# The causal mask inside VectorE's scan, and the carried product without GpSimd: stick-breaking attention in a hybrid decoder layer

## The chip, the core and the metric

The kernel runs on one core of a Trainium2 chip. The metric is the device time of one execution in microseconds (us), from several runs of each kernel on the same chip; smaller is better. The engines are TensorE (PE; PEld are its weight loads), VectorE (DVE), ScalarE (ACT) and GpSimd (POOL); SyncE (SP) issues most DMAs, GpSimd those that feed the attention.

## What is computed

One layer over a prompt of 2048 tokens with 16 meta tokens before them, and over 8 sequences that each add 8 tokens to a cache of 512. A norm, one input projection, then side by side a stick-breaking attention (8 heads of 64) and a gated linear recurrence; an output projection, a norm, an MLP of squared ReLU, a norm. The attention is what the change touches:

```python
z = einsum(q, k) * HEAD_DIM**-0.5 + bias
mask = k_pos[None, :] < q_pos[:, None]
log_keep = where(mask, log_sigmoid(-z), 0.0)
suffix = lax.cumsum(log_keep, axis=3, reverse=True) - log_keep
w = where(mask, exp(log_sigmoid(z) + suffix), 0.0)
out = einsum(w, v)
```

A key's weight is sigmoid(z) times the product of (1 - sigmoid(z')) over all later keys that the query may see. A query sees neither its own key nor later ones.

## The kernel before

The sequence is four blocks `s` of 512 tokens. For each block the projections run first (`inproj`: recurrence, keys, values, queries), and the attention of finished blocks is mixed into later work: `attn` and `sample_attn` are generators, and each GEMM hands them a little time after every few of its products (`work.tick`, with rates written out by hand). TensorE's order is exactly the order in which the program is written; a scheduler orders the other engines. Matrix products take three passes each (high by high, low by high, high by low, lines 181 to 183 and 213 to 215), and the weights are split on the way: ScalarE casts the high part (L158), VectorE subtracts the low part (L159).

In `attn`, work goes head by head and from the latest group of 512 keys to the earliest. For a 128-row tile of queries, `logits` (L692) makes two products into a PSUM tile S (L696). Where the tile holds the rows' own keys, a third product adds -2^100 to the masked places: the identity `identb` times the table `maskb`, both bf16 (L698). There are 4 such tiles for each head of each block, 128 in all. Then `chain` (L629) has ScalarE compute keep = sigmoid(-z) and beta = sigmoid(z) (L634, L635). VectorE scans keep from the last key to the first, each element the product so far (L643), into `pb`, starting from 1 or from the `carry` of the later group, and multiplies beta with the scan's element one place to the right (L646). That one place further, the last column of `pb`, is filled by GpSimd: a memset of 1 (L637) or a copy of the carry (L640). GpSimd also copies the scan's end into a new `carry` (L645). `chain` runs 360 times: 352 times for the prompt, 8 times for the samples. Some steps later the weights are transposed (L707), split on ScalarE and VectorE (L718, L719) and multiplied with the values (L729, L731). When a head is done, its output goes through a tile taken from the two buffers of `keep` (L738 to L741) to memory.

The buffers bound how far things run ahead: 3 PSUM tiles for logits and transposes, 2 each of `keep` and `pb`, 9 of beta. GpSimd's queue, which runs in order, holds these small copies, the loads of queries, keys and values (L661 to L686), the cache pages of the samples (L827), the memset of L713 before each group's last transpose, the gate arithmetic of the recurrence (L455, L525 to L529), the copy of the recurrence's state (`hcar`, L481), and the norms' powers (L237).

Of the kernel before, what the change touches and what calls it, by code (L numbers as in the profile page):

```python
# [84 lines left out]
def _program(tc, I, O, NSB, NSC):  # L85
# [194 lines left out]
    def consts(p1, gt):  # L280
# [9 lines left out]
        identb = C([P, P], BF16, "identb")  # L290
        nc.gpsimd.tensor_copy(identb, ident)
        mk = T(p1, [P, P], F32, "spad", 2)
        nc.sync.dma_start(mk, I["mask"])
        maskb = C([P, P], BF16, "maskb")
        nc.gpsimd.tensor_copy(maskb, mk)
        st["identb"], st["maskb"] = identb, maskb
# [9 lines left out]
        tmp = C([P, NH], F32, "tmph")  # L306
# [29 lines left out]
        e = C([P, 4], F32, "sp_e")  # L336
        m = C([P, 4], F32, "sp_m")
        nl = C([P, 4], F32, "sp_nl")
# [4 lines left out]
        d = C([P, 4], F32, "sp_d")  # L343
        nc.vector.tensor_scalar(d, e, 2.0, None, op0=ALU.add)
        nc.vector.reciprocal(d, d)
        t = C([P, 4], F32, "sp_t")
        nc.vector.tensor_tensor(t, e, d, op=ALU.mult)
        t2 = C([P, 4], F32, "sp_t2")
        nc.vector.tensor_tensor(t2, t, t, op=ALU.mult)
        q = C([P, 4], F32, "sp_q")  # L350
# [81 lines left out]
    def inproj(s, p1, pa, K, ahi, alo, before_k=None):  # L432
# [27 lines left out]
        def recur(cs):  # L460
# [7 lines left out]
            for c in cs:  # L468
# [12 lines left out]
                nc.gpsimd.tensor_copy(K["hcar"][:, c:c + 1], hs[:, NP - 1:NP])  # L481
# [145 lines left out]
    WB = 9  # L627

    def chain(S, n, bias, nbias, carry):  # L629

        beta = T(att, [P, 512], F32, "beta", WB)
        keep = T(att, [P, 512], F32, "keep", 2)
        pb = T(att, [P, 513], F32, "pb", 2)
        nc.scalar.activation(keep[:, 0:n], S, AF.Sigmoid, bias=nbias, scale=-0.125)  # L634
        nc.scalar.activation(beta[:, 0:n], S, AF.Sigmoid, bias=bias, scale=0.125)  # L635
        if carry is None:
            nc.gpsimd.memset(pb[:, n:n + 1], 1.0)  # L637
            init = 1.0
        else:
            nc.gpsimd.tensor_copy(pb[:, n:n + 1], carry)  # L640
            init = carry
        kr = keep[:, 0:n][:, ::-1]
        nc.vector.tensor_tensor_scan(pb[:, 0:n][:, ::-1], kr, kr, init, op0=ALU.mult, op1=ALU.bypass)  # L643
        cn = T(att, [P, 1], F32, "carry", 12)
        nc.gpsimd.tensor_copy(cn, pb[:, 0:1])  # L645
        nc.vector.tensor_tensor(beta[:, 0:n], beta[:, 0:n], pb[:, 1:n + 1], op=ALU.mult)  # L646
        return beta, cn


    def attn(s, K):  # L650
# [41 lines left out]
        def logits(H, h, i, kap, n, mask):  # L692
            S = psT()
            o = S[:, 0:n]
            for e in range(2):
                nc.tensor.matmul(o, H["q"][:, e, i * P:(i + 1) * P], kap, start=(e == 0), stop=(e == 1 and mask is None))  # L696
            if mask is not None:
# [593 lines left out]
```

## Time and profile before

| | |
|---|---|
| median of 3 runs | 2803.51 us (2800.16 to 2811.13) |
| the profiled execution's own time | 2806.19 us |
| its span, first to last instruction | 2804.3 us |
| mean granted clock of TensorE | 0.986 |
| ScalarE, GpSimd busy | 1451.3 us (52%), 748.9 us (27%) |

The profile shows one execution. The projections of the first block fill the time to some 430 us, with the samples' attention from 180 us on. The prompt's attention runs from 432 to 2160 us beside the other projections and the MLP; after that the MLP is alone. Matrix products are pipelined: a duration reaches into the next instruction, and how much room one takes is read from start to start.

### The profile page before, as it was taken

The page shows a single profiled execution, that of the slowest core. Times are in us where ns is not written, and L with a number is a line of the kernel's source. Part 1 is how long each engine was busy: PE and PEld are TensorE (multiplying, and loading weights), DVE is VectorE, ACT ScalarE, POOL GpSimd, SP SyncE. Part 2 cuts the span into 40 slices and gives each one's busy share as a digit, 9 for nine tenths or more (in the row PEclk, how much of TensorE's full clock was granted, in tenths as well). Part 3 has the DMA queues.
Part 4 walks back from the last instruction along what each step waited for, and adds up shares of the span by engine and source line. Part 5 has one row for each costly group of instructions (what it writes and reads, how often), then busy time and mean ns, then how long its engine had stood idle before and what let it go on. Part 6 is the DMA issues. An engine that isn't in the chain of part 4 may idle for free.

```text
span 2804.3 us, 38592 instructions
## 1 busy us (share of the span) xinstructions
PE 2698.7 (96%) x13932; PEld 2216.3 (79%) x13932; DVE 1789.9 (64%) x2412; ACT 1451.3 (52%) x2426; POOL 748.9 (27%) x1447
## 2 busy tenths in 40 slices
PE   8999987998899999999999999999999999999998
PEld 7886756776688888887888888878888887998996
DVE  6455364776776777788867777787676436333434
ACT  6466364675665655566555555565555234332332
POOL 5336372442332322233222222442221002000002
PEclk9999998999999999999999999999999999999999
DMA  5465845567534443345543333454333334222223
GB/s 169 133 205 189 267 138 163 145 174 209 166 95 123 119 116 108 107 132 153 154 116 108 107 108 107 129 167 136 103 96 103 113 121 143 96 82 78 82 83 113
DMA packets 177471, 368.39 MB, mean 131 GB/s; under 512 B 49169, under 2 KB 79505, under 8 KB 177281
## 3 DMA queue, kind: packets, MB, share of 16 engines
q1 hardware_dynamic: 103936, 287.41, 32.4%
q0 software_dynamic: 73344, 78.52, 11.3%
q8 instruction: 110, 1.80, 0.3%
q14 instruction: 81, 0.66, 0.1%
HBM read 305.58 MB, written 60.04 MB: 130 GB/s over the span
## 4 chain that ended last, share of the span: by engine, by line
PE 78%; DVE 7%; DMA 5%; POOL 4%; issue 3%; ACT 3%; SPq 0%; DVEq 0%; POOLq 0%; ACTq 0%
PE D L181 11%; PE D L182 10%; PE D L183 10%; PE D L213 10%; PE D L214 10%; PE D L215 10%; PE T L707 4%; PE T L696 4%; PE O L729 2%; PE O L731 2%; DVE pb L643 1%; DMA vd<-vst 1%; DVE wlo L159 1%; POOL rstd L237 1%; DMA q<-qd 1%
## 5 line engine op out<-in xcount | busy, mean ns | idle before, releaser
L159 DVE TENSOR_TENSOR wlo<-wraw,whi 128x1024 fp32r<-128x1024 f32 x368 | 466.1, 1267 | 495.4 <-ACT whi L158 490.0
L181 PE MATMUL D<-ahi,whi 128*128 128x512 f32 (+3 forms) x1920 | 711.8, 371 | 0.7 <-ACT ahi L1012 0.7
L183 PE MATMUL D<-ahi,wlo 128*128 128x512 f32 (+3 forms) x1920 | 686.0, 357 | 2.5 <-DVE wlo L159 2.5
L182 PE MATMUL D<-alo,whi 128*128 128x512 f32 (+3 forms) x1920 | 686.3, 357 | 1.6 <-DVE alo L1013 1.6
L158 ACT CAST whi<-wraw 128x1024 fp32r<-128x1024 f32 x368 | 386.3, 1050 | 477.8 <-PE D L214 285.3
L213 PE MATMUL D<-whi,uh 128*128 128x512 f32 x1024 | 418.6, 409 | 0.0
L183 PEld LDWEIGHTS D<-ahi,wlo 128*128 128x128 f32 x1920 | 364.3, 190 | 54.3 <-DVE wlo L159 3.9
L181 PEld LDWEIGHTS D<-ahi,whi 128*128 128x128 f32 x1920 | 365.2, 190 | 52.8 <-issue 9.1
L214 PE MATMUL D<-whi,ul 128*128 128x512 f32 x1024 | 404.3, 395 | 0.0
L215 PE MATMUL D<-wlo,uh 128*128 128x512 f32 x1024 | 403.9, 394 | 0.0
L182 PEld LDWEIGHTS D<-alo,whi 128*128 128x128 f32 x1920 | 365.5, 190 | 44.3 <-DVE alo L1013 1.8
L634 ACT ACTIVATE keep<-T,nbias 128x512 f32<-128x512 f32 (+6 forms) x352 | 209.9, 596 | 254.2 <-PE T L696 148.2
L643 DVE TENSOR_TENSOR_SCAN pb<-keep,carry 128x512 f32<-128x512 f32 (+1 forms) x228 | 267.7, 1174 | 70.8 <-ACT keep L634 67.6
L645 POOL COPY carry<-pb 128x1 f32<-128x1 f32 x360 | 93.5, 260 | 569.0 <-DVE pb L643 560.5
L719 DVE TENSOR_TENSOR wtl<-T,wth 128x512 fp32r<-128x512 f32 (+1 forms) x320 | 190.6, 602 | 75.2 <-ACT wth L718 74.5
L718 ACT CAST wth<-T 128x512 fp32r<-128x512 f32 (+1 forms) x320 | 166.1, 523 | 122.0 <-PE T L707 118.8
L215 PEld LDWEIGHTS D<-wlo,uh 128*128 128x128 f32 x1024 | 192.2, 188 | 46.7
L646 DVE TENSOR_TENSOR beta<-beta,pb 128x512 f32<-128x512 f32 (+7 forms) x360 | 209.1, 581 | 31.0 <-POOL carry L645 1.5
L213 PEld LDWEIGHTS D<-whi,uh 128*128 128x128 f32 x1024 | 192.7, 188 | 39.4 <-DVE uf L1028 0.5
L214 PEld LDWEIGHTS D<-whi,ul 128*128 128x128 f32 x1024 | 192.9, 188 | 38.3
L635 ACT ACTIVATE beta<-T,bias 128x512 f32<-128x512 f32 (+6 forms) x352 | 208.4, 592 | 0.0
L707 PE MATMUL T<-ident,beta 128*128 128x128 f32 (+1 forms) x1216 | 192.4, 275 | 12.5 <-ACT beta L635 8.6
(237 smaller groups left out, 3907.5 us busy)
## 6 DMA issues: line engine op xcount, KB each, us to landing
wraw<-in_w_up SPq DMA_DIRECT2D x128, 512.0 KB, 3.5
wraw<-in_w_down SPq DMA_DIRECT2D x128, 512.0 KB, 3.5
wraw<-in_w_in SPq DMA_DIRECT2D x64, 512.0 KB, 4.0
q<-qd POOLq DMA_DIRECT2D x32, 512.0 KB, 17.0
wraw<-in_w_out SPq DMA_DIRECT2D x32, 512.0 KB, 3.6
kv<-kd POOLq DMA_DIRECT2D x48, 256.0 KB, 3.8
kv<-vd POOLq DMA_DIRECT2D x48, 256.0 KB, 4.5
y<-in_x_prompt SPq DMA_DIRECT2D x16, 512.0 KB, 6.1
```

The costliest lines, as they stand in the source:

```text
L158: nc.scalar.copy(hi, r)
L159: nc.vector.tensor_tensor(lo, r, hi.bitcast(F32), op=ALU.subtract)
L181: nc.tensor.matmul(o, whi[:, k, :], ahi(k, a, b), start=(k == 0), stop=False)
L182: nc.tensor.matmul(o, whi[:, k, :], alo(k, a, b), start=False, stop=False)
L183: nc.tensor.matmul(o, wlo[:, k, :], ahi(k, a, b), start=False, stop=(k == KC - 1))
L213: nc.tensor.matmul(o, h, whi[:, kk, :], start=st, stop=False)
L214: nc.tensor.matmul(o, l, whi[:, kk, :], start=False, stop=False)
L215: nc.tensor.matmul(o, h, wlo[:, kk, :], start=False, stop=sp)
L634: nc.scalar.activation(keep[:, 0:n], S, AF.Sigmoid, bias=nbias, scale=-0.125)
L643: nc.vector.tensor_tensor_scan(pb[:, 0:n][:, ::-1], kr, kr, init, op0=ALU.mult, op1=ALU.bypass)
L646: nc.vector.tensor_tensor(beta[:, 0:n], beta[:, 0:n], pb[:, 1:n + 1], op=ALU.mult)
L707: nc.tensor.transpose(t[0:kn, i * P:(i + 1) * P], w[:, c0:c0 + kn], ident)
```

## The change

The mask product and its two tables go, and so does their load. In their place stands one constant, `own`, 513 columns of zeros with the identity in columns 384 to 511. For a tile that holds the rows' own keys the scan starts from 0 and adds `own` at each step: it stays 0 until the row's own key, becomes 1 there, and is the product of keep from there on. `keep` is now two fixed tiles of 513 columns whose last column is set to 1 once; results stand against the right end, and the scan takes one more element, which puts the start value itself into `pb`. So the memset and the copy into `pb` are gone from GpSimd, and the copies of `carry` and of `hcar` are VectorE's. The head's output goes through a buffer of `pb`. Small tiles of a set-up computation share one buffer, which moves nothing that the rest speaks of.

```diff
-        identb = C([P, P], BF16, "identb")
-        nc.gpsimd.tensor_copy(identb, ident)
-        mk = T(p1, [P, P], F32, "spad", 2)
-        nc.sync.dma_start(mk, I["mask"])
-        maskb = C([P, P], BF16, "maskb")
-        nc.gpsimd.tensor_copy(maskb, mk)
+        own = C([P, 513], BF16, "own")
+        nc.gpsimd.memset(own, 0.0)
+        nc.gpsimd.tensor_copy(own[:, 384:512], ident)
...
-                nc.gpsimd.tensor_copy(K["hcar"][:, c:c + 1], hs[:, NP - 1:NP])
+                nc.vector.tensor_copy(K["hcar"][:, c:c + 1], hs[:, NP - 1:NP])
...
-    def chain(S, n, bias, nbias, carry):
-
+    def chain(S, n, bias, nbias, carry, own=None):
+        if not keeps:
+            for i in range(2):
+                keeps.append(T(att, [P, 513], F32, f"keep{i}"))
+                nc.vector.memset(keeps[i][:, 512:513], 1.0)
+        keep = keeps[turn[0] % 2]
+        turn[0] += 1
+        o = 512 - n
         beta = T(att, [P, 512], F32, "beta", WB)
-        keep = T(att, [P, 512], F32, "keep", 2)
         pb = T(att, [P, 513], F32, "pb", 2)
-        nc.scalar.activation(keep[:, 0:n], S, AF.Sigmoid, bias=nbias, scale=-0.125)
+        nc.scalar.activation(keep[:, o:512], S, AF.Sigmoid, bias=nbias, scale=-0.125)
         nc.scalar.activation(beta[:, 0:n], S, AF.Sigmoid, bias=bias, scale=0.125)
-        if carry is None:
-            nc.gpsimd.memset(pb[:, n:n + 1], 1.0)
-            init = 1.0
+        kr = keep[:, o:513][:, ::-1]
+        if own is not None:
+            nc.vector.tensor_tensor_scan(pb[:, o:513][:, ::-1], kr, own[:, o:513][:, ::-1], 0.0 if carry is None else carry,
+                                         op0=ALU.mult, op1=ALU.add)
         else:
-            nc.gpsimd.tensor_copy(pb[:, n:n + 1], carry)
-            init = carry
-        kr = keep[:, 0:n][:, ::-1]
-        nc.vector.tensor_tensor_scan(pb[:, 0:n][:, ::-1], kr, kr, init, op0=ALU.mult, op1=ALU.bypass)
+            nc.vector.tensor_tensor_scan(pb[:, o:513][:, ::-1], kr, kr, 1.0 if carry is None else carry,
+                                         op0=ALU.mult, op1=ALU.bypass)
         cn = T(att, [P, 1], F32, "carry", 12)
-        nc.gpsimd.tensor_copy(cn, pb[:, 0:1])
-        nc.vector.tensor_tensor(beta[:, 0:n], beta[:, 0:n], pb[:, 1:n + 1], op=ALU.mult)
+        nc.vector.tensor_copy(cn, pb[:, o:o + 1])
+        nc.vector.tensor_tensor(beta[:, 0:n], beta[:, 0:n], pb[:, o + 1:513], op=ALU.mult)
...
-            if mask is not None:
-                nc.tensor.matmul(S[:, mask:mask + P], K["identb"], K["maskb"], start=False, stop=True)
...
-                of = T(att, [P, SB], F32, "keep", 2)[0:64]
+                of = T(att, [P, 513], F32, "pb", 2)[0:64, 0:SB]
```

The order of the instructions moves at three places. On TensorE, in a head of the first block, a masked logits tile stood before a group's transposes:

```order
L696 MATMUL T_5397<-kv_4911,q_5274 128x144 x2
L698 LDWEIGHTS identb_179
L698 MATMUL T_5397<-maskb_183,identb_179 128x128
L707 MATMUL T_5411<-ident_72,beta_5045 128x128
L707 MATMUL T_5411<-ident_72,beta_5106 128x128
L707 MATMUL T_5411<-ident_72,beta_5178 128x128
L181 MATMUL D_5378<-ahi_101,whi_5287 128x512
```

and in a head of the first block now (lines of the changed kernel: L702 is the product of L696, L712 the transpose of L707):

```order
L702 MATMUL T_5302<-kv_4833,q_5182 128x144 x2
L712 MATMUL T_5313<-ident_72,beta_4960 128x128
L712 MATMUL T_5313<-ident_72,beta_5018 128x128
L712 MATMUL T_5313<-ident_72,beta_5088 128x128
L181 MATMUL D_5283<-ahi_101,whi_5195 128x512
```

The weight load and the product of L698 are gone, 128 times, and nothing else on TensorE has another place. Of the 128, 64 had transposes right behind them, 58 a GEMM product (one of the values among them), and 6 the next tile's logits.

On VectorE, in the norms of the first output projection (L740 adds the two halves of a head's output, L980 is the norm's gain), before:

```order
L643 SCALAR_TENSOR_TENSOR pb_6776<-keep_6775,carry_6624 128x512
L646 TENSOR_TENSOR beta_6774<-beta_6774,pb_6776 128x512
L740 TENSOR_TENSOR keep_6797<-O_6533,keep_6797 64x512
L643 SCALAR_TENSOR_TENSOR pb_6809<-keep_6808,carry_6661 128x400
L646 TENSOR_TENSOR beta_6807<-beta_6807,pb_6809 128x400
L159 TENSOR_TENSOR wlo_6837<-wraw_6761,whi_6836 128x1024
```

and now (L648 is the scan without a mask, L651 the carry, L652 the product with beta, L745 the head's output):

```order
L648 SCALAR_TENSOR_TENSOR pb_6607<-keep_294_1890,carry_6465 128x513
L651 COPY carry_6611<-pb_6607 128x1
L652 TENSOR_TENSOR beta_6606<-beta_6606,pb_6607 128x512
L745 TENSOR_TENSOR pb_6627<-O_6377,pb_6627 64x512
L648 SCALAR_TENSOR_TENSOR pb_6638<-keep_293_1888,carry_6499 128x401
L651 COPY carry_6642<-pb_6638 128x1
L652 TENSOR_TENSOR beta_6637<-beta_6637,pb_6638 128x400
L159 TENSOR_TENSOR wlo_6663<-wraw_6593,whi_6662 128x1024
```

One copy of one column stands between each scan and its product; apart from that VectorE's order is nearly the same.

On GpSimd, in the recurrence of the second block (L529 is the last of a gate's steps, L455 the next gate's first, L713 the memset), before:

```order
L529 TENSOR_TENSOR gt_5427<-gt_5427,g_5425 128x512
L645 COPY carry_5460<-pb_5455 128x1
L640 COPY pb_5524<-carry_5336 128x1
L645 COPY carry_5490<-pb_5485 128x1
L637 MEMSET pb_5603 128x1
L455 TENSOR_TENSOR ii_5509<-ii_5509,xc_5367 128x512
L713 MEMSET wth_5537 128x512
```

and now, under the line numbers 528, 454 and 718:

```order
L528 TENSOR_TENSOR gt_5329<-gt_5329,g_5327 128x512
L454 TENSOR_TENSOR ii_5405<-ii_5405,xc_5272 128x512
L718 MEMSET wth_5431 128x512
```

Every wait of GpSimd for a scan or for a product with beta has left its queue.

## Rows read from the trace of the kernel before

**Rows 1.** The page, part 1: busy time of an engine, its share of the span and its instructions.

```profile
PE 2698.7 (96%) x13932; PEld 2216.3 (79%) x13932; DVE 1789.9 (64%) x2412; ACT 1451.3 (52%) x2426; POOL 748.9 (27%) x1447
```

**Rows 2.** Busy time by stretch, whole program. Columns: the stretch and its length in us; then for TensorE (PE), its weight loads (PEld), VectorE (DVE), ScalarE (ACT) and GpSimd (POOL) the busy us with the number of instructions in brackets; then the granted clock as a share of full speed, the busy share of the DMA engines, and GB/s.

```profile
430.00:830.00 400.00, 356.44 (x1708) 284.82 (x1707) 275.76 (x395) 238.10 (x426) 139.74 (x308) 0.94 0.57 162
830.00:1300.00 470.00, 470.00 (x2298) 386.70 (x2297) 354.44 (x471) 272.09 (x472) 130.03 (x319) 1.00 0.43 119
1300.00:1360.00 60.00, 52.96 (x266) 42.09 (x265) 54.28 (x76) 35.87 (x64) 23.98 (x45) 1.00 0.63 197
1360.00:1860.00 500.00, 499.61 (x2410) 409.04 (x2409) 376.68 (x485) 285.81 (x483) 132.96 (x310) 1.00 0.40 117
...
1900.00:2170.00 270.00, 270.00 (x1302) 221.79 (x1301) 197.73 (x251) 152.78 (x250) 54.18 (x136) 1.00 0.35 105
```

**Rows 3.** The same stretches, for the mask product of line 698 alone (PE, PEld, then granted clock, DMA share and GB/s).

```profile
430.00:830.00 400.00, 12.07 (x51) 5.08 (x51) 0.94 0.57 162
830.00:1300.00 470.00, 8.51 (x37) 3.55 (x37) 1.00 0.43 119
...
1360.00:1860.00 500.00, 6.21 (x27) 2.59 (x27) 1.00 0.40 117
...
1900.00:2170.00 270.00, 2.76 (x12) 1.15 (x12) 1.00 0.35 105
```

**Rows 4.** Timeline of TensorE around one masked logits tile of 512 columns that a GEMM follows. Columns: start, duration in us, engine, line, operation; a duration runs into the next one, so the pace is read from the starts.

```profile
710.82 0.63 PE L696 MATMUL T<-kv,q 128*128 128x512 f32 x2
711.29 0.23 PE L698 MATMUL T<-maskb,identb 128*128 128x128 bf16 x1
711.33 0.48 PE L213 MATMUL D<-whi,ahi 128*128 128x512 f32 x1
711.64 0.39 PE L214 MATMUL D<-whi,alo 128*128 128x512 f32 x1
```

**Rows 5.** The same for an unmasked logits tile of 512 columns that a GEMM follows.

```profile
1506.21 0.63 PE L696 MATMUL T<-kv,q 128*128 128x512 f32 x2
...
1506.91 0.39 PE L182 MATMUL D<-alo,whi 128*128 128x512 f32 x1
```

**Rows 6.** A masked tile of 512 columns that four transposes follow: its two products, and the first GEMM product behind the transposes.

```profile
1231.33 0.62 PE L696 MATMUL T<-kv,q 128*128 128x512 f32 x2
...
1232.22 0.48 PE L213 MATMUL D<-whi,ahi 128*128 128x512 f32 x1
```

**Rows 7.** The unmasked twin of rows 6.

```profile
1003.36 0.63 PE L696 MATMUL T<-kv,q 128*128 128x512 f32 x2
...
1004.18 0.48 PE L213 MATMUL D<-whi,uh 128*128 128x512 f32 x1
```

**Rows 8.** The chain that ended last, in order of time, from 225 to 252 us: start, duration, what.

```profile
228.81 1.13 POOL hcar L481
...
243.53 0.13 POOL hcar L481
...
245.12 4.15 DMA kv<-in_cache_v,ix
...
249.32 0.65 PE O L879 x8
```

**Rows 9.** Timeline of GpSimd around 592 us; in square brackets the idle time before an instruction and what ended it.

```profile
590.46 1.28 POOL L529 TENSOR_TENSOR gt<-gt,g 128x512 f32<-128x512 f32 x1 [0.74 <-ACT gt L528]
...
593.88 2.08 POOL L455 TENSOR_TENSOR ii<-ii,xc 128x512 f32<-128x512 f32 x1
595.90 0.52 POOL L713 MEMSET wth<- 128x512 f32 x1
```

**Rows 10.** The one TensorE instruction of the stretch 597 to 599.2 us.

```profile
598.95 0.50 PE L729 MATMUL O<-wth,kv 128*128 128x512 f32 x1 [2.07 <-DVE wth L715]
```

**Rows 11.** Timeline of VectorE in the norms of the first output projection.

```profile
741.88 0.42 DVE L643 TENSOR_TENSOR_SCAN pb<-keep 128x128 f32<-128x128 f32 x1
742.40 0.29 DVE L646 TENSOR_TENSOR beta<-beta,pb 128x128 f32<-128x128 f32 x1
...
755.62 0.14 DVE L233 TENSOR_SCALAR ms<-ss 128x1 f32<-128x1 f32 x1
755.68 0.15 DVE L235 SCALAR_TENSOR_TENSOR ms<-ss,ss 128x1 f32<-128x1 f32 x1
755.75 0.55 DVE L646 TENSOR_TENSOR beta<-beta,pb 128x384 f32<-128x384 f32 x1
```

**Rows 12.** Busy time by stretch for the scan of line 643 alone (DVE, then clock, DMA share, GB/s).

```profile
430.00:830.00 400.00, 67.68 (x78) 0.94 0.57 162
...
1300.00:1360.00 60.00, 9.71 (x9) 1.00 0.63 197
```

**Rows 13.** Costliest groups by line and shape: instructions, busy us and mean ns of one, idle time before them and what ended it.

```profile
L643 DVE TENSOR_TENSOR_SCAN pb<-keep,carry 128x512 f32<-128x512 f32 x124 | 158.9, 1281 | 37.5 <-ACT keep L634 35.8 <-POOL pb L640 0.7
...
L640 POOL COPY pb<-carry 128x1 f32<-128x1 f32 x228 | 128.4, 563 | 144.8 <-DVE beta L646 138.6 <-DVE ms L235 3.2 <-POOL carry L645 0.8
```

**Rows 14.** The recurrence scan of line 479, from the view of that line: count, then minimum, median and maximum duration in ns, first and last start in us, forms.

```profile
L479 DVE TENSOR_TENSOR_SCAN ii<-r,hcar,b x12: 1282/1284/2292, 208.1 to 603.6; 128x512 f32<-128x512 f32 x12
```

**Rows 15.** The write of a head's output, line 741: who waited for it (us, times), and its time from issue to landing.

```profile
  ACT keep L634: 9.0, 5
...
DMA to landing us min/median/max: 2.2/4.3/11.5
```

More of the change, by code (lines that the diff above doesn't have):

```diff
@@ L289, in consts @@
         st["g_pre"], st["g_mlp"] = gt[:, 0], gt[:, 1]
-        identb = C([P, P], BF16, "identb")
-        nc.gpsimd.tensor_copy(identb, ident)
-        mk = T(p1, [P, P], F32, "spad", 2)
-        nc.sync.dma_start(mk, I["mask"])
-        maskb = C([P, P], BF16, "maskb")
-        nc.gpsimd.tensor_copy(maskb, mk)
-        st["identb"], st["maskb"] = identb, maskb
+        own = C([P, 513], BF16, "own")
+        nc.gpsimd.memset(own, 0.0)
+        nc.gpsimd.tensor_copy(own[:, 384:512], ident)
+        st["own"] = own
         maskS = C1([P, 4, NSAMP], F32, "maskS")
@@ L334, in consts @@
         st["gw"] = gw
-        e = C([P, 4], F32, "sp_e")
-        m = C([P, 4], F32, "sp_m")
-        nl = C([P, 4], F32, "sp_nl")
+        e = tiny[:, 0, :]
+        m = tiny[:, 1, :]
+        nl = tiny[:, 2, :]
         nc.vector.tensor_scalar(nl, lam, -1.0, None, op0=ALU.mult)
@@ L690, in attn, with logits @@
         groups = [(h, g) for h in range(NH) for g in range(s, -1, -1)]
-        def logits(H, h, i, kap, n, mask):
+        def logits(H, h, i, kap, n, diag):
             S = psT()
@@ L695, in logits @@
             for e in range(2):
-                nc.tensor.matmul(o, H["q"][:, e, i * P:(i + 1) * P], kap, start=(e == 0), stop=(e == 1 and mask is None))
-            if mask is not None:
-                nc.tensor.matmul(S[:, mask:mask + P], K["identb"], K["maskb"], start=False, stop=True)
-            w, H["carry"][i] = chain(S[:, 0:n], n, K["bias"][:, h:h + 1], K["nbias"][:, h:h + 1], H["carry"][i])
+                nc.tensor.matmul(o, H["q"][:, e, i * P:(i + 1) * P], kap, start=(e == 0), stop=(e == 1))
+            w, H["carry"][i] = chain(S[:, 0:n], n, K["bias"][:, h:h + 1], K["nbias"][:, h:h + 1], H["carry"][i],
+                                     K["own"] if diag else None)
             live["w"] += 1
@@ L763, in s_items @@
                         yield None
-                    wtop = logits(H, h, 3, H["kt"][:, 0:P], P, 0)
+                    wtop = logits(H, h, 3, H["kt"][:, 0:P], P, True)
                     yield 0.6
@@ L770, in s_items @@
                     kap = kvt[:, 0:m]
-                    mask = m - P if (g == s and i < 3) else None
                     while live["w"] >= WB:
                         yield None
-                    ws.append(logits(H, h, i, kap, m, mask))
+                    ws.append(logits(H, h, i, kap, m, g == s and i < 3))
                     if i < 3:
@@ L1245, in layout @@
     i = np.arange(P)
-    A["mask"] = np.where(i[None, :] >= i[:, None], np.float32(BIG), np.float32(0)).astype(np.float32)
     ms = np.full((P, 4, NSAMP), BIG, np.float32)
```

12 lines of the change are left out of this document (7 added, 5 removed).

## The prediction

> **What bounds the kernel now.** I read the page first: TensorE is busy in 96% of the span, VectorE in 64% [rows 1]. A share is an average, so the next view is busy time by stretch [rows 2]. The reader is to see two kinds of stretch. From 830 to 1300, 1360 to 1860 and 1900 to 2170 us TensorE is busy for 470 of 470, 499.6 of 500 and 270 of 270 us at full granted clock; VectorE has a quarter of that time free (354.4 of 470, 376.7 of 500, 197.7 of 270). There the end is set by TensorE's instructions alone: one that goes, goes from the time, and what VectorE gains costs nothing. From 430 to 830 us TensorE is busy for only 356.4 of 400, at a mean granted clock of 0.94 between its levels of 2.4 and 1.2 GHz; it waits for others, and work taken from it partly becomes a longer wait. In 1300 to 1360 us, the norms of the second output projection, VectorE is busy for 54.3 of 60 us and sets the pace.
>
> **The mask product.** It stands 51 times in the disturbed stretch, 37, 27 and 12 times in the three full ones, and once between: 76 fully on the path [rows 3]. A product's printed duration runs into the next, so I take its room from starts. Masked, 512 columns, GEMM behind it: from the logits' first product at 710.82 to the second product of the GEMM at 711.64 is 0.82 us [rows 4]. Unmasked it is 1506.21 to 1506.91, 0.70 us [rows 5]. The mask takes 0.12 us, three times its own slot of 711.29 to 711.33: the product behind it starts 0.31 us before its successor (711.33 to 711.64) and not 0.23. With transposes behind, the masked stretch takes 1231.33 to 1232.22, 0.89 us [rows 6], the unmasked one 1003.36 to 1004.18, 0.82 us [rows 7]: 0.07. Half of the masks have transposes behind them, so the mean of the two, 0.095, would be the price; but of a head's four masked tiles, by the code 128, 256, 384 and 512 columns wide, three are narrower, and a short product leaves less time in which the next weights can be loaded. No narrow tile without a mask stands in the trace to show it, so I take 0.11, with 0.07 and 0.13 as ends. The 76 give 76 x 0.11 = 8.4 us (5.3 to 9.9). The other 52 would give 5.7; with TensorE waiting in 11% of that stretch, behind waits that end when they end, I count 60% of it, 3.4 us (0 to 6.8). Sum 11.8 us.
>
> The Trainium skill, "TensorE: Matmul & The Clock Gate", section "Back-to-back issue gap", gives another price: 128 columns divided by 2.4 GHz plus 2.5 ns, 56 ns, or 81 ns for a load and its product in a sustained stream. By it 128 masks would be an estimated 7 to 10 us wherever they stand, in place of my 11.8, and the time 2 to 5 us higher, inside the forecast's own range. The trace agrees behind transposes (0.07) and not where a GEMM follows (0.12).
>
> **GpSimd's queue.** It loses 360 + 228 + 132 small instructions, 16 copies of `hcar`, and their waits. Most of that was beside TensorE's work. Twice it was not. From 228.81 us the chain that ended last runs along GpSimd and contains the `hcar` copies, 1.13 us and 0.13 us, before the load of a cache page at 245.12, for which TensorE's products of line 879 wait until 249.32 [rows 8]. These 1.3 us go from in front of the load; what is late next is the gate arithmetic in the same queue, so no more than that. At 592 us the gate step of line 529 ends at 591.74, and line 455 begins at 593.88; four of the removed instructions stand between them in the order shown above. So line 455, and the memset of line 713 at 595.90 behind it, can come up to 2.1 us sooner [rows 9], and TensorE waited 2.07 us for what hangs on that memset [rows 10]. I count 2.0. Together 3.3 us (0 to 5; next late is ScalarE, which must have the gate's sigmoid ready).
>
> One rule speaks against this term. "Perfetto Trace Analysis" of the Trainium skill, section "Optimizing Scalar/DVE Operations", says that VectorE and GpSimd share an SBUF port, so that moving work between those two might not help. By the rule the term would be 0 and the sum 10.2. No run here shows the copies on VectorE yet; on GpSimd the one-column copy of line 640 takes a mean of 563 ns [rows 13].
>
> **VectorE's copies.** It gets 360 + 16 copies of one column and two memsets, each in front of other VectorE work. A one-column instruction of VectorE prints 0.14 us, but the next begins 0.06 to 0.07 us later (755.62, 755.68, 755.75) [rows 11]: 378 x 0.067 = 25 us of VectorE. A copy reads what the scan just wrote, and pays the wait that the product paid until now: it began 0.10 us after the scan's end (741.88 + 0.42 to 742.40), where independent work overlaps [rows 11]. The product behind the copy no longer waits for that, so the copy adds its slot and not a second wait. In the full stretches the quarter of free VectorE time hides it. In 1300 to 1360 us with 9 scans it is 9 x 0.067 = 0.6 us on the path. Of the 78 scans from 430 to 830 us [rows 12], 5.2 us, I count a fifth, because VectorE is busy for 275.8 of 400 us there. Sum 1.6 us against the change (0 to 6).
>
> **What I cost at nothing.** The masked scan multiplies and adds with a second tensor instead of one. The nearest row is the recurrence scan, which does that over 512 columns in a median of 1284 ns [rows 14]; the unmasked scan takes 1281 [rows 13]. A bf16 second operand stands in no row. Bounds: nothing, or half again for 128 scans of at most 1.3 us, 83 us of VectorE, mostly covered by its free quarter and worth 5 us at the waits. One more column is 1/512 of 1.28 us. The head's output now holds a buffer of `pb`, so scans wait for its write, where ScalarE's keep waited before, 9.0 us in 5 cases, with a landing time of 2.2 to 11.5 us [rows 15]. The scan comes later than the keep, so the wait should shrink; it stands in VectorE's queue with weight splits behind it, so I leave 3 us for a loss and 2 for a gain. At the start a mask load and two GpSimd casts become a memset and a cast: 1 us either way.
>
> **The sum.** 11.8 + 3.3 - 1.6 = 13.5 us off the profiled execution's 2806.2 us, which is 2792.7; that execution lies 2.7 us over the median of the runs, so the median comes to 2790.0, 0.48% less.
>
> **Rivals.**
> The mask costs its slot alone. What follows a mask slows down after any change of the kind of product, also without it: the GEMM product behind the transposes prints 0.48 us in rows 6 and in rows 7 alike. If in most places the slow restart stays, the 76 give 76 x 0.05 = 3.8 us, the disturbed ones 1, and with half of GpSimd's term and VectorE's 1.6 against it the gain is 5 us: 2798. Against it: rows 4 and 5.
>
> The disturbed stretches heal. TensorE stands 43.6 us idle from 430 to 830 us, and a clock of 0.94 costs 6% of 400, 24 us [rows 2]. If a freer GpSimd, and logits that reach ScalarE 0.1 us sooner, take away a quarter of both, 17 us come on top of the full-stretch masks, the cache page and the copies: 8.4 + 17 + 1.3 - 1.6 = 25 us, 2778. For it: GpSimd is on the chain there. Against: most of these idle times end with loads and norms that the change leaves alone.
>
> Scans wait for the head's output. This one ends on the other side. If the scan meets the write's whole landing time at each of the 32 heads, VectorE stands still for 32 x 4.3 = 138 us in pieces, with weight splits queued behind; once a piece passes the slack of the split weights, TensorE stops too. At 1 us of TensorE for each head that is 32 us: 2790 + 32 = 2822. It decides from 0.9 us a head on. Against it: ScalarE met that write 5 times only.
>
> That the change doesn't do what it says would be mask products still standing on TensorE; the order shows none, so I give it nothing.
>
> **Chances and range.** My forecast 0.52, the slot alone 0.22, the healing 0.22, the waiting scans 0.04. A measurement of this kernel tells about 0.5% from no change, 14.0 us: below 2789.5 is faster, above 2817.5 slower. The forecast's own range, 2784 to 2796, straddles the first line: 0.24 of its chance lies below it. Faster 0.24 + 0.22 = 0.46; same 0.28 + 0.22 = 0.50; slower 0.04. The range for 8 in 10 runs from 2777, most of the healing, to 2801, the slot alone with its own copies.
>
> **What would show it.** In the changed profile: no instruction of line 698, and TensorE's busy time down by some 12 us or more. From a masked tile's first product to the second GEMM product behind it 0.70 us at 512 columns. Copies that begin 0.1 us after their scan, products 0.07 us after the copy. The wait for the cache page at 249 us ending a good 1 us sooner, and no wait of TensorE for the memset near 599 us. VectorE up by 25 us. I am wrong if the full stretches together shrink by less than 5 us, if TensorE waits in them, or if VectorE shows waits for the write of a head's output of more than 20 us.

## The result, and the profile after

The changed kernel takes 2785.7 us, median of 6 runs (2782.32 to 2790.22), beside 2805.4 us (2800.16 to 2812.00) for the kernel before on the same chip: a ratio of 0.9923, with a 95% interval of 0.9908 to 0.9938. By that ratio it is 21.6 us less (17.4 to 25.8), 0.77%, and more than the 0.5% that can be told from no change; the two medians lie 19.7 us apart. The forecast was 13.5 us, 0.48%. So sign and range were right, and some 8 us of the gain were not in the sum. One execution of a kernel below (the output in `wtl`), 2954.90 us at a granted clock of 0.845, is left out of its ratio.

The profiled execution of the changed kernel, 2790.22 us, was the longest of its six; its span is 2788.3 us. The page, part 1, which answers to [rows 1]:

```profile
PE 2688.2 (96%) x13804; PEld 2219.4 (80%) x13804; DVE 1814.3 (65%) x2790; ACT 1451.6 (52%) x2426; POOL 515.5 (18%) x711
```

TensorE has 128 products less and 10.5 us less to do, VectorE 378 instructions and 24.4 us more, GpSimd 736 instructions and 233 us less.

Since TensorE's order is the same in both kernels but for the mask products, every other product has a twin, and a stretch can be cut at the same product in both traces. Busy time by stretch of the changed kernel, cut at the twins of the products that began at 830.17, 1300.13, 1360.18, 1860.08, 1900.26 and 2170.00 us before (columns as in [rows 2]):

```profile
827.16:1293.74 466.58, 466.58 (x2261) 386.33 (x2259) 361.73 (x576) 272.08 (x472) 65.24 (x113) 1.00 0.42 120
1293.74:1354.99 61.25, 54.93 (x265) 44.51 (x264) 54.42 (x84) 35.62 (x64) 18.79 (x25) 0.94 0.62 195
1354.99:1851.93 496.94, 496.65 (x2382) 408.69 (x2381) 383.33 (x588) 286.55 (x485) 61.36 (x107) 1.00 0.40 117
...
1888.84:2157.41 268.57, 268.57 (x1289) 221.50 (x1288) 200.74 (x303) 153.05 (x250) 18.88 (x37) 1.00 0.35 106
```

These rows show that TensorE is still busy all through the three full stretches, and that these became 469.96 - 466.58, 499.90 - 496.94 and 269.74 - 268.57, together 7.5 us shorter. The stretch of the norms from 1300 to 1360 us went the other way: 61.25 us in place of 60.05, at a granted clock of 0.94 and not 1.00.

The twins of [rows 4] and of [rows 6], TensorE's timeline (columns as there):

```profile
708.02 0.62 PE L702 MATMUL T<-kv,q 128*128 128x512 f32 x2
708.49 0.40 PE L213 MATMUL D<-whi,ahi 128*128 128x512 f32 x1
708.72 0.39 PE L214 MATMUL D<-whi,alo 128*128 128x512 f32 x1
...
1225.32 0.62 PE L702 MATMUL T<-kv,q 128*128 128x512 f32 x2
1225.78 0.60 PE L712 MATMUL T<-ident,beta 128*16 128x128 f32 x4
1226.14 0.48 PE L213 MATMUL D<-whi,ahi 128*128 128x512 f32 x1
```

First product to second GEMM product: 0.70 us, where it was 0.82. Logits to the first GEMM product behind the transposes: 0.82, where it was 0.89. Both as the unmasked twins had promised. Taken over all 76 masks of the full stretches, twin by twin, the 36 with transposes behind saved a mean of 0.067 us, the 40 others (37 with a GEMM product behind, 3 with the next tile's logits) 0.128; together 7.5 us, 0.099 each.

VectorE's timeline at the twin of [rows 11]'s scan:

```profile
738.99 0.41 DVE L645 TENSOR_TENSOR_SCAN pb<-keep,own 128x129 f32<-128x129 f32 x1
739.44 0.15 DVE L651 COPY carry<-pb 128x1 f32<-128x1 f32 x1
739.51 0.28 DVE L652 TENSOR_TENSOR beta<-beta,pb 128x128 f32<-128x128 f32 x1
```

The copy begins 0.04 us after the scan's end, the product 0.07 us after the copy. From the scan's start to the product's it is 0.52 us, as it was before (741.88 to 742.40): behind a scan with nothing in between the copy fits into the gap that was there anyway.

The scans by shape (columns as in [rows 13]):

```profile
L648 DVE TENSOR_TENSOR_SCAN pb<-keep,carry 128x513 f32<-128x513 f32 x124 | 160.7, 1296 | 37.4 <-ACT keep L640 36.6
...
L645 DVE TENSOR_TENSOR_SCAN pb<-keep,own 128x513 f32<-128x513 f32 x24 | 30.4, 1268 | 7.8 <-ACT keep L640 5.8 <-DMA md<-pb 1.6
```

The scan that masks takes 1268 ns, the plain one 1296: the second operand in bf16 costs nothing.

### The profile page after: what moved, and what is told of

Same layout as the page of the kernel before. It is cut to its first block, busy times and chain, and to the rows that moved or that the text cites. A ratio compares the mean times of both kernels' runs of the same rounds, so it can differ in the third digit from the quotient of the medians.

```text
span 2788.3 us, 36998 instructions
## 1 busy us (share of the span) xinstructions
PE 2688.2 (96%) x13804; PEld 2219.4 (80%) x13804; DVE 1814.3 (65%) x2790; ACT 1451.6 (52%) x2426; POOL 515.5 (18%) x711
## 3 DMA queue, kind: packets, MB, share of 16 engines
q0 software_dynamic: 73344, 78.52, 11.3%
## 4 chain that ended last, share of the span: by engine, by line
PE 80%; DVE 7%; DMA 5%; POOL 3%; issue 3%; ACT 2%; SPq 0%; POOLq 0%; DVEq 0%; ACTq 0%
PE D L181 11%; PE D L183 11%; PE D L182 11%; PE D L213 10%; PE D L214 10%; PE D L215 10%; PE T L712 4%; PE T L702 4%; PE O L734 2%; PE O L736 2%; DVE wlo L159 1%; DMA md<-pb 1%; DVE pb L648 1%; POOL rstd L237 1%; DMA q<-qd 1%
## 5 line engine op out<-in xcount | busy, mean ns | idle before, releaser
L648 DVE TENSOR_TENSOR_SCAN pb<-keep,carry 128x513 f32<-128x513 f32 (+1 forms) x228 | 270.3, 1186 | 71.9 <-ACT keep L640 69.9
L652 DVE TENSOR_TENSOR beta<-beta,pb 128x512 f32<-128x512 f32 (+7 forms) x360 | 208.2, 578 | 0.0
L712 PE MATMUL T<-ident,beta 128*128 128x128 f32 (+1 forms) x1216 | 193.7, 277 | 14.1 <-ACT beta L641 7.6
L702 PE MATMUL T<-kv,q 128*128 128x512 f32 (+5 forms) x640 | 180.4, 364 | 10.3 <-ACT beta L641 4.4
```

Of the source, the lines that this page charges most:

```text
L648: nc.vector.tensor_tensor_scan(pb[:, o:513][:, ::-1], kr, kr, 1.0 if carry is None else carry, op0=ALU.mult, op1=ALU.bypass)
L712: nc.tensor.transpose(t[0:kn, i * P:(i + 1) * P], w[:, c0:c0 + kn], ident)
```

## What became of GpSimd's term

GpSimd's timeline at the twin of [rows 9], and the TensorE instruction that answers to [rows 10]:

```profile
589.76 1.29 POOL L528 TENSOR_TENSOR gt<-gt,g 128x512 f32<-128x512 f32 x1 [0.74 <-ACT gt L527]
593.18 2.03 POOL L454 TENSOR_TENSOR ii<-ii,xc 128x512 f32<-128x512 f32 x1 [2.13 <-ACT ii L453]
595.16 0.52 POOL L718 MEMSET wth<- 128x512 f32 x1
```

```profile
598.18 0.50 PE L734 MATMUL O<-wth,kv 128*128 128x512 f32 x1 [2.01 <-DVE wth L720]
```

The four small instructions are gone, and line 454 still stands idle for 2.13 us: ScalarE has not got the gate's sigmoid ready. TensorE's wait is 2.01 us where it was 2.07. The 2.0 us that I counted here were not there.

## The experiments

Two questions: is the mask as large as I made it, and where do the other 8 us come from? Theory A had the mask as the larger half of the gain; theory B the disturbed stretches, first through GpSimd's queue (B1), then through the buffer of the head's output (B2). Each ratio is to the kernel before, run beside it on the same chip, with its 95% interval; us are the ratio's distance from 1 times the median of the kernel before. The distance of the two medians differs from it by some 4 us at most. Every diff below shows only the lines that matter, "..." marks a cut.

**The mask alone** (kernel before; starts from 0 or from the carry as written by GpSimd):

```diff
-            if mask is not None:
-                nc.tensor.matmul(S[:, mask:mask + P], K["identb"], K["maskb"], start=False, stop=True)
...
+            nc.vector.tensor_tensor_scan(pb[:, 0:n][:, ::-1], kr, own[:, 512 - n:512][:, ::-1], init,
+                                         op0=ALU.mult, op1=ALU.add)
```

> The mask inside the scan, all of GpSimd's copies kept. Theory A (the mask product is the larger half: 76 products in the full stretches at the 0.10 us that the aligned traces give, 7.5 us, and some 3 us of the 52 others): 9 to 12 us off, ratio about 0.996, and the full stretches shrink as in the changed kernel. Theory B (the waits of the disturbed stretches, shortened by GpSimd's empty queue, bring most): 7 to 8 us off, ratio 0.997 or above, nothing from the stretches where TensorE waits.

0.9959 (0.9946 to 0.9972): 11.5 us (7.9 to 15.2). The predicted 11.8 us stand, with a wide interval. The trace shows less: twin by twin the 76 masks take the same 0.126 us (GEMM behind) and 0.066 us (transposes) with them, but the full stretches shrink by 5.8 us and not by the 7.5 that theory A expected, so something else in them became longer; and 2.2 of the 8.7 us that its last product is ahead lie before 180 us, where no mask stands.

**All but the mask** (changed kernel, with the mask product of line 698 back and scans that start from 1):

```diff
+            if diag:
+                nc.tensor.matmul(S[:, n - P:n], K["identb"], K["maskb"], start=False, stop=True)
```

> The carry, the start value and the recurrence's state off GpSimd, the mask product kept on TensorE. Theory A: 3 to 6 us off (ratio 0.998 to 0.999), since only the cache page and the memset chain gain. Theory B: 10 to 14 us off (ratio 0.995 to 0.9965), as much as the changed kernel gained beyond the 7.5 us of the full stretches. In both the full stretches keep their length within 1 us.

0.9944 (0.9925 to 0.9963): 15.7 us (10.4 to 21.1). The predicted value of this part was 3.3 - 1.6 = 1.7 us, and that is outside. This part and the mask alone add up to 27.2 us where the whole change has 21.6; the intervals are wide enough for that, and a stretch in which it may lie comes below.

**Each mask product twice** (kernel before; a second, idle mask product):

```diff
+                nc.tensor.matmul(S[:, mask:mask + P], K["identb"], K["maskb"], start=False, stop=False)
```

> The kernel before with every mask product issued twice (the second adds the same table again). If the first product's price is mostly the change of kind of product, the second costs only its slot, 0.05 to 0.06 us: 128 more cost 4 to 7 us (ratio 1.0015 to 1.0025). If each mask product takes 0.10 us by itself, 8 to 13 us (1.003 to 1.0045).

1.0009 (0.9996 to 1.0021). The end moves by less than the scatter; the full stretches tell more: they grew by 2.08, 1.75 and 0.72 us, 0.060 for each of 76. TensorE's timeline shows why a second one is cheaper than the first:

```profile
707.96 0.63 PE L696 MATMUL T<-kv,q 128*128 128x512 f32 x2
708.43 0.23 PE L698 MATMUL T<-maskb,identb 128*128 128x128 bf16 x1
708.49 0.22 PE L699 MATMUL T<-maskb,identb 128*128 128x128 bf16 x1
708.52 0.48 PE L213 MATMUL D<-whi,ahi 128*128 128x512 f32 x1
708.84 0.40 PE L214 MATMUL D<-whi,alo 128*128 128x512 f32 x1
```

The second adds its 0.06 us of room; the slow product behind it (0.32 us from 708.52 to 708.84, and not 0.23) stands there once, as with one mask. So of 0.099 us some 0.06 are the mask's own room and 0.04, as a mean, what it does to its neighbour: 0.07 where a GEMM product follows and 0.01 where transposes do. The rival "the slot alone" (0.05) falls for the first kind; for the second it nearly holds.

**The head's output in the tiles of `keep`** (changed kernel, the last line of the diff undone, as far as the fixed tiles let it):

```diff
-                of = T(att, [P, 513], F32, "pb", 2)[0:64, 0:SB]
+                of = keeps[turn[0] % 2][0:64, 0:SB]
+                turn[0] += 1
```

> The changed kernel with the head's output in a buffer of keep, as before, and not of pb. If scans behind the output's write cost anything, this is 2 to 6 us faster than the changed kernel (ratio 0.990 to 0.9915); if the scan comes late enough, it is the same as the changed kernel, 0.992, or a little slower, because ScalarE waits again.

0.9988 (0.9977 to 0.9999): all but 3.4 us of the gain is gone. The view of the write's line, who waited for it and its time to landing:

```profile
  ACT keep L640: 55.4, 19
...
DMA to landing us min/median/max: 2.2/3.8/11.7
```

ScalarE waits 55.4 us in 19 cases where it waited 9.0 in 5 before [rows 15], with about the same landing times. The buffer is now needed by the second tile behind the output in most of the cases, where the waits of the kernel before (at 608 and 632 us) stand at the third. TensorE then waits for ScalarE's beta (from all waits of TensorE; columns: us in total, times, longest):

```profile
PE T L712 <- ACT beta L641: 15.2, 7, 5.4
PE T L702 <- ACT beta L641: 13.6, 3, 6.6
```

In the changed kernel these two are 7.6 and 4.4 us. This run undoes more than one line of the change and so can't price it; what it shows is that the place of this one buffer can be worth the whole gain. The run of that line alone, below, prices it.

**The changed kernel again.**

> The changed kernel once more, to see which stretches differ between its executions. All theories: ratio 0.992. Its profile should lie 2 to 5 us under the first one (2788.3 us), most of it before 180 us, where the first execution's input loads came late.

0.9925 (0.9912 to 0.9937), 21.1 us: the result repeats.

**GpSimd's copies back** (changed kernel, with one GpSimd copy for each scan, into a tile that nobody reads):

```diff
         nc.vector.tensor_copy(cn, pb[:, o:o + 1])
+        idle = T(att, [P, 1], F32, "idle", 2)
+        nc.gpsimd.tensor_copy(idle, pb[:, o:o + 1])
```

> The changed kernel with one copy on GpSimd for each scan again (the carry into a tile that nobody reads; VectorE's copy stays). Theory B1 (GpSimd's queue, stopped behind scans, made the disturbed stretches long): most of the 8 to 12 us that the changed kernel gained there come back, ratio 0.995 to 0.9965. Theory B2 (it was the buffers: where the head's output and keep lie, and not GpSimd): within 2 us of the changed kernel, 0.9915 to 0.993.

0.9925 (0.9913 to 0.9937): no difference. GpSimd's queue stands behind 360 scans again, and the end doesn't move. So B1 falls for the copies of the carry; the memsets and copies into `pb`, in front of the scans, did not come back in this run. What the copies do in parts comes below.

**The head's output in `pb`, alone** (kernel before):

```diff
-                of = T(att, [P, SB], F32, "keep", 2)[0:64]
+                of = T(att, [P, 513], F32, "pb", 2)[0:64, 0:SB]
```

> The kernel before with the head's output in a buffer of pb and nothing else. Theory B2: 4 to 10 us faster than before (0.9965 to 0.9985). Theory B1, and the prediction's cost of nothing: same as before within 2 us (0.9993 to 1.0007).

0.9983 (0.9973 to 0.9993): 4.8 us (2.0 to 7.6). I had costed this edit at nothing. Who waited for the write now:

```profile
  POOL pb L637: 32.2, 7
  POOL pb L640: 14.9, 11
  DVE pb L643: 11.3, 4
```

The waits are longer in sum, 58 us against 9, but ScalarE, whose keep leads to everything behind it, is free of them. In the trace 3.4 us of the gain lie from 430 to 830 us, 1.2 of them from 610 to 660 us, around ScalarE's longest wait before (5.67 us, to 631.66); 2.4 us lie before 180 us, where no head's output is written yet, and are scatter. That ScalarE's freedom is the cause fits this and is not shown beyond it.

**The recurrence's state on VectorE, alone** (kernel before; `hcar` copied by VectorE):

```diff
-                nc.gpsimd.tensor_copy(K["hcar"][:, c:c + 1], hs[:, NP - 1:NP])
+                nc.vector.tensor_copy(K["hcar"][:, c:c + 1], hs[:, NP - 1:NP])
```

> The kernel before with the copy of the recurrence's state on VectorE and nothing else. The prediction's term for the cache page: 1 to 2 us faster (0.9993 to 0.9997), all of it between 180 and 430 us. If these 16 copies held up more than that: 4 us or more (0.9985 or less).

0.9985 (0.9973 to 0.9997): 4.2 us (0.8 to 7.6), with medians only 2.2 us apart. The trace doesn't say where: its twins are 1.25 us ahead at the end, and from 180 to 250 us, where the copies stood on the chain [rows 8], they gain nothing. My 1.3 us are inside the interval and not where I put them. GpSimd's timeline shows why; before, and behind it without the copies:

```profile
228.75 1.19 POOL L481 COPY hcar<-ii 128x1 f32<-128x1 f32 x1
229.89 1.76 POOL L529 TENSOR_TENSOR gt<-gt,g 128x512 f32<-128x512 f32 x1
```

```profile
228.53 1.50 POOL L529 TENSOR_TENSOR gt<-gt,g 128x512 f32<-128x512 f32 x1 [0.74 <-ACT gt L528]
...
236.14 0.51 POOL L500 COPY xp<-convc 128x3 f32<-128x3 f32 x1 [3.08 <-DVE xc L508]
```

Without the copy, line 529 stands for ScalarE's sigmoid, and line 500 stands 3.08 us for VectorE in both kernels. From the start of the gate step ahead of the first copy to the load of the cache page behind the second it is 17.05 us before (226.75 to 243.80) and 16.97 without them (225.73 to 242.70): 0.1 us, and not 1.3.

**Mask and buffer together** (kernel before with both edits; everything of GpSimd stays):

```diff
+            nc.vector.tensor_tensor_scan(pb[:, 0:n][:, ::-1], kr, own[:, 512 - n:512][:, ::-1], init,
+                                         op0=ALU.mult, op1=ALU.add)
...
+                of = T(att, [P, 513], F32, "pb", 2)[0:64, 0:SB]
```

> The kernel before with two parts of the change: the mask in the scan, and the head's output in a buffer of pb. GpSimd keeps its memsets, its copies into pb, of the carry and of hcar, and VectorE gets no copies. Theory S (the parts add): 11.5 + 4.8 = 16 us, ratio 0.994, and the remaining 5 us of the change come with the state's copy and the start value that the scan writes itself. Theory M (mask and buffer are all of it, the rest is scatter): 21 us, ratio 0.9925, as the whole change. Theory O (the two gains overlap, since both shorten ScalarE's waits in the first blocks): 11 us, ratio 0.996.

0.9943 (0.9930 to 0.9956): 16.0 us (12.3 to 19.6), beside 11.5 + 4.8 = 16.3. These two parts add, and the rest of the whole change, 5 us (about 0 to 10), is left for the start value that the scan writes (and the fixed tiles of `keep` that go with it) and for the copies that left GpSimd.

**Against the scan's wait.** In the changed kernel one wait of VectorE stands out, for the write of the second head's output. VectorE's timeline, and then TensorE's:

```profile
500.75 0.55 DVE L724 TENSOR_TENSOR wtl<-T,wth 128x384 fp32r<-128x384 f32 x1
507.90 0.73 DVE L645 TENSOR_TENSOR_SCAN pb<-keep,own 128x273 f32<-128x273 f32 x1 [6.60 <-DMA md<-pb]
...
509.08 0.42 DVE L724 TENSOR_TENSOR wtl<-T,wth 128x256 fp32r<-128x256 f32 x1
```

```profile
509.56 0.66 PE L261 MATMUL T<-ident,y 128*128 128x128 f32 x4 [2.85 <-DVE wtl L724]
```

The scan stands still for 6.60 us, the weights behind it in VectorE's queue (line 724 at 509.08) are late, and TensorE waits for them. The changed kernel's second execution has the same wait, 6.55 us; the profile names `keep` as its end there, but that `keep` had been ready for 5.1 us. Two edits of the changed kernel follow: the output in one of the three buffers of `wtl`, and the write issued by GpSimd. The first:

```diff
-                of = T(att, [P, 513], F32, "pb", 2)[0:64, 0:SB]
+                of = T(att, [P, SB], F32R, "wtl", 3).bitcast(F32)[0:64]
```

> The changed kernel, with the head's output in one of the three buffers of wtl (the low part of the transposed weights) in place of one of pb, so that no scan needs the buffer of a write that has not landed. Theory W (a scan's wait for the output's write is what the change still loses): the 6.6 us wait of the scan at 507.9 us goes, the 4.1 us lost between 480 and 530 us in two executions of the changed kernel become 0 or a small gain, VectorE waits less than 3 us for such writes in all, and the ratio to the kernel before falls from 0.9925 to about 0.991. Theory T (the loss at 480 to 530 us is the low clock there, and the wait only happens to lie in it): the loss stays at 3 us or more, and the ratio stays at 0.9925. Should the buffers of wtl be the tighter ones, VectorE or ScalarE waits for the write as often as before, and the ratio rises to 0.994 or more.

0.9910 (0.9891 to 0.9930). A ratio of 0.991 was expected, but the interval holds 0.9925 too, and theory W's place is only half right: the loss between 480 and 530 us shrinks from 4.1 us to 2.6, since line 724 needs its buffer early as well:

```profile
506.28 0.42 DVE L724 TENSOR_TENSOR wtl<-T,wth 128x256 fp32r<-128x256 f32 x1 [3.88 <-DMA md<-wtl]
```

The second edit, the write issued by GpSimd:

```diff
-                nc.sync.dma_start(md[s][64 * (h % 2):64 * (h % 2) + 64, h // 2, :], of)
+                nc.gpsimd.dma_start(md[s][64 * (h % 2):64 * (h % 2) + 64, h // 2, :], of)
```

> The changed kernel, with the write of a head's output issued by GpSimd in place of SyncE. Theory L (the write lands late because it stands behind SyncE's loads and stores): the write issued near 496.6 us lands in 6 us or less in place of 11.2, the scan's wait of 6.6 us shrinks to 2 or less, the loss between 480 and 530 us goes, ratio about 0.991. Theory W (what is in flight from all queues shares the DMA engines, and the distance of the buffer decides): that landing stays above 8 us, the loss stays, ratio 0.9925; it may get worse, if GpSimd's own queue issues the write late, 0.995.

0.9991 (0.9982 to 1.0000): the gain is gone. GpSimd's timeline, and VectorE's behind it:

```profile
502.56 0.57 POOL L746 DMA_DIRECT2D md<-pb  x1
```

```profile
514.50 0.72 DVE L645 TENSOR_TENSOR_SCAN pb<-keep,own 128x273 f32<-128x273 f32 x1 [7.48 <-DMA md<-pb]
```

The landing takes some 12 us on this queue too, where three loads stand right ahead of it, and not the 6 us or less of theory L: SyncE's queue alone was not what made it late. Besides, GpSimd now waits for the output itself, 23.5 us in 19 cases, with its loads queued behind; the stretch from 610 to 660 us alone loses 9.2 us. How the loss divides between these waits and the scans' (24.7 us in 4 cases) is not shown.

**The output in `wtl`, and the copy of the carry on GpSimd:**

```diff
-        nc.vector.tensor_copy(cn, pb[:, o:o + 1])
+        nc.gpsimd.tensor_copy(cn, pb[:, o:o + 1])
```

> The changed kernel with the head's output in a buffer of wtl, as in the run beside it, and with the copy of the carry on GpSimd again: VectorE loses 360 copies, 24 us of its time, and GpSimd waits for scans as in the kernel before. If the copies are hidden on VectorE as predicted (1.6 us of 25 on the path), this comes out within 2 us of the run beside it, ratio about 0.991. If VectorE's time is worth more in the disturbed stretches, 0.989 or less. If GpSimd's queue behind the scans matters after all, 0.993 or more.

0.9918 (0.9905 to 0.9931), 2787.6 us beside 2787.8: 360 copies on VectorE or on GpSimd, the end is the same. None of these versions can be told from the changed kernel.

## Stretch by stretch

The same end can hide gains and losses. The us that each stretch of the kernel before (by its own time) became shorter, from the starts of twin products:

| stretch | mask only | mask, buffer | all but mask | changed | again | GpSimd copies back | `wtl` | `wtl`, carry on GpSimd |
|---|---|---|---|---|---|---|---|---|
| 330 to 430 | -0.4 | -0.6 | 2.5 | 2.4 | 2.2 | -0.2 | 3.0 | -1.0 |
| 480 to 530 | 0.0 | -0.1 | 0.8 | -4.1 | -4.2 | 1.0 | -2.6 | 1.4 |
| three full ones | 5.8 | 6.6 | 0.2 | 7.5 | 7.6 | 6.9 | 7.2 | 5.9 |
| 1300 to 1360 | -0.2 | 0.1 | -1.4 | -1.2 | -2.2 | -2.4 | -2.3 | 0.6 |
| 1860 to 1900 | 0.6 | 0.5 | 3.8 | 3.3 | 1.7 | 3.4 | 2.1 | 3.4 |

Three things sort the columns.

*GpSimd without a copy for each scan.* The columns without one gain 2 to 3 us from 330 to 430 us, the others nothing. But three of these four lose 2.6 to 4.2 us from 480 to 530 us, at the wait for the write of the second head's output. From that write's issue to the start of the instruction that waited it is 11.3 us in these three. In the fourth (all but mask), which loses nothing, and in the columns with GpSimd's copies back and with the carry on GpSimd it is 8.4 to 8.6 us. The loads and stores issued around it are the same in nearly the same order, so what makes it land later is not shown. The gain and the loss about cancel, which fits that 360 GpSimd copies cost nothing in the end. The loss is also one that neither the mask alone nor all but the mask has, so it may be why these two add up to more than the whole.

*Copies on VectorE.* In the norms from 1300 to 1360 us the seven traces with them take 60.7 to 62.5 us, the seven without 59.0 to 60.3: means 61.7 and 59.7, 2 us where I had counted 0.6. Of the seven without, only the changed kernel with the output in `wtl` and the carry on GpSimd (last column) differs from the changed kernel in little else. Its busy time in this stretch; behind it that of the kernel with `wtl` and the copies on VectorE, and of the kernel before with the output in `pb`:

```profile
1288.51:1347.93 59.42, 52.94 (x264) 42.10 (x263) 54.19 (x76) 35.88 (x64) 21.91 (x34) 1.00 0.64 200
```

```profile
1288.65:1350.96 62.31, 54.02 (x265) 43.28 (x263) 54.34 (x84) 35.59 (x64) 18.79 (x25) 0.97 0.64 191
```

```profile
1294.61:1353.62 59.01, 53.99 (x265) 43.37 (x264) 54.04 (x76) 35.81 (x64) 25.21 (x46) 0.97 0.64 201
```

VectorE is busy for about as long with the copies as without (54.34 and 54.19), so a longer VectorE is not what the 2 us are. The clock granted in this stretch is 0.92 to 0.97 with them and 0.97 to 1.00 without, but the last two rows have the same clock and nearly the same TensorE time and differ by 3.3 us of TensorE's idle time. How the copies cost 2 us is open.

*The start value that the scan itself writes.* From 1860 to 1900 us, the norms after the MLP, all eight traces with it take 36.6 to 38.7 us, the six others 39.3 to 40.5: 2.6 us by the means. The kernel before there; behind it the changed kernel, and the one with everything changed but the mask:

```profile
1860.08:1900.50 40.42, 36.27 (x177) 29.22 (x176) 38.58 (x50) 25.15 (x44) 17.55 (x29) 0.96 0.53 164
```

```profile
1851.93:1889.08 37.15, 34.50 (x177) 27.99 (x175) 36.66 (x57) 24.59 (x43) 11.45 (x11) 1.00 0.54 174
```

```profile
1850.91:1887.54 36.63, 34.31 (x177) 28.01 (x176) 36.15 (x57) 24.06 (x42) 11.43 (x11) 1.00 0.53 170
```

GpSimd has 11 instructions here where it had 29; its copies into `pb` stood in one queue with the norms' arithmetic. A part of the difference is the clock: at a granted 0.96 the stretch takes 40.2 us without and 38.5 with it (five and two traces), at 1.00 39.3 and 37.1 (one and six), so at one clock some 2 us. I had put no term on this stretch. Since GpSimd's copies of the carry, put back, leave the gain at 3.4, it is not the copy behind the scan that matters here. By elimination it is the copy into `pb` in front of it, or the fixed tiles of `keep` that go with the new start; no run has one without the other.

## Why the prediction was right, and where it failed

*What bounds the kernel* held for the full stretches: TensorE's instructions set them, and in the changed kernel the room of those that went is gone from the time. That VectorE sets the pace from 1300 to 1360 us is not borne out: the stretch changed by 2 us while VectorE's busy time stayed the same.

*The mask product, 11.8 us*, held: 11.5 us (7.9 to 15.2) alone. The price was a little high. The two rows gave 0.12 and 0.07, the measured means are 0.128 and 0.067, and their plain mean of 0.095 would have been nearer to 0.099 than the 0.11 that I chose for fear of narrow tiles. Narrow tiles cost hardly more: with a GEMM product behind, a mask took 0.08, 0.14, 0.13 and 0.13 us on tiles of 128, 256, 384 and 512 columns, with transposes 0.05, 0.07, 0.08 and 0.08. TensorE's busy time fell by 10.5 us, a little less than the 12 that I had named as a sign. The page "TensorE: Matmul & The Clock Gate" of the Trainium skill, section "Back-to-back issue gap", gives 56 ns for a product of 128 columns by itself, and 81 ns where each product has its weight load. The second mask product, which has a load of its own, took 0.060 us, nearer to the first figure. The first mask product cost 0.099 us, since it also slows what follows.

*GpSimd's queue, 3.3 us*, had about the right size by chance and was wrong in its places. The 2.0 us at line 455 failed: the step took the removed instructions for the cause of an idle time that ScalarE ends, though it named ScalarE as next late. The 1.3 us in front of the cache page were not there either: 0.1 us with `hcar` alone, since what was late next was not, as I wrote, the gate arithmetic in the same queue but ScalarE and VectorE, for which that arithmetic waits. The product behind the cache page does come sooner in the two executions of the changed kernel, by 1.8 and 0.9 us from 225 us on, but by 0.0 with `hcar` alone. In their place came 2.6 us from 1860 to 1900 us, and 2 to 3 us from 330 to 430 us, with a loss of 4 us from 480 to 530 us against them.

*VectorE's copies, -1.6 us*: 25 us of VectorE forecast, 24.4 measured, hidden in the full stretches as predicted. The 0.6 us of 1300 to 1360 us were 2, and not as busy time of VectorE.

The rule of "Perfetto Trace Analysis" of the Trainium skill, section "Optimizing Scalar/DVE Operations", that such a move might not help, agrees with the end for the copies of the carry: on VectorE or on GpSimd they give 0.9910 and 0.9918, and copies on GpSimd in addition leave 0.9925 at 0.9925. That a shared port is the reason, no run shows.

*What I cost at nothing* is the step that failed. "I leave 3 us for a loss and 2 for a gain" for the buffer of the head's output: measured alone it is a gain of 4.8 us (2.0 to 7.6). I had compared how long the waits would be, and not who waits. ScalarE's 9.0 us stood in front of everything that follows keep, and 58 us of GpSimd and VectorE cost less than they did; that the path runs through ScalarE's wait is my reading, and the runs show only the price. Put right with this term alone, the sum is 13.5 + 4.8 = 18.3 us, inside the interval of the result. So the total came within its range partly by luck: the two gains that I had placed at GpSimd were not there, and others that I had not seen took their place. The masked scan did cost nothing.

*The rivals.* "The slot alone" fell with the twins (0.099), though behind transposes (0.067) it was not far off. "The disturbed stretches heal": 17 us more did not come; a few us did, at two places, and half of them were lost again. "Scans wait for the head's output" did not decide: VectorE waits in the changed kernel (view of the write's line) for

```profile
  DVE pb L645: 14.5, 5
...
  DVE pb L648: 0.2, 1
...
DMA to landing us min/median/max: 2.2/3.8/11.9
```

14.7 us, under the 20 that I had set. But its mechanism is real: the stretch with the longest such wait is 4 us longer, and a buffer that is needed one tile sooner, or a write issued from GpSimd's queue, loses nearly all of the gain.

*What stays open*: how the copies on VectorE make 1300 to 1360 us longer; where `hcar` alone gains its 4 us, if it does; why the second head's write lands 3 us later in three of the kernels; and whether the wait near 507 us can be removed. No run gives the head's output a tile of its own.

## What to carry to other kernels

Price an instruction in a full stretch by the starts of its twins with and without it, by what follows it: the row was right, the correction to it was not. When a DMA's source buffer moves to another ring, ask first who will wait and what stands behind the waiter, and only then for how long. Before counting an idle time as the work of removed instructions, find what releases the instruction behind it when they are gone.

## What the runs showed of the hardware

A second bf16 product of the same kind as the one ahead of it took 0.060 us of room, while the first of its kind between fp32 products cost a mean of 0.099: 0.128 where mostly GEMM products follow, 0.067 where transposes do. A scan of 513 columns that adds a bf16 second operand runs as fast as one that only multiplies (means of 1268 and 1296 ns). The write of a head's output, 128 KB, took 2.2 to 11.9 us to land in the changed kernel, where SyncE issues it, and 2.3 to 14.1 when GpSimd did.
